# A gate matrix on its way through DRAM: eight groups of four expert blocks side by side behind the partition

## The chip, the cores and the metric

One core of one Trainium2 chip runs the program. The time is that of the device for one execution, in microseconds; lower is better. The kernel before was run three times (1939.65, 1940.6 and 1941.2 us, median 1940.6 us), and one more execution was profiled.

## The reference, cut to what matters

One decoder layer over 512 tokens of width 1024: a recurrent mixer and a sparse attention, merged; then a layer of 16,384 experts of which each token uses 8 heads x 16; then an embedding gate and a norm. The change lies in the layer of experts. For a token `t` with input `x`, expert scores are sums of two key scores, the best 16 of each head are kept, and their softmax is the gate:

```python
def peer_ffn(x, w_q, sub_keys, u_tab, v_tab):
    ...
    e_idx = (jnp.take_along_axis(i1, ci // PEER_TOPK, axis=-1) * N_KEYS +
             jnp.take_along_axis(i2, ci % PEER_TOPK, axis=-1))
    g = jax.nn.softmax(best, axis=-1).astype(x.dtype)
    ...
        act = jax.nn.gelu(jnp.einsum('cd,chkd->chk', xc, u)) * gc
        v = v_tab[ec]
        return jnp.einsum('chk,chkd->cd', act, v)
```

An expert is named by two numbers of 0 to 127: its block `e` (128 blocks of 128 experts) and its place in the block.

## The kernel before

The tokens stand in four tiles of 128. For three of them (384 tokens, `ND`) the kernel doesn't gather experts: it computes the activation of every expert for every token, `gelu(x u)`, block by block, multiplies it by a gate matrix G that is zero except at the chosen experts, and multiplies the result by the table `v`. For the fourth tile (`GT`) it gathers rows of both tables with indirect DMAs from GpSimd.

Three things run side by side from 798 to 1186 us, in one order written out by hand for each engine:

- *The activations of the blocks,* `xu_fill` (L1085): for each block `e`, a load of the table on SyncE's queue (L1060), a split into a high and a low part on ScalarE (`uh`, L1065) and VectorE (`ul`, L1070), 24 matmuls (`xu`), the gelu on ScalarE (`ac`, L1080), and a store of `ac` to `xdram` from ScalarE's queue (L1097).
- *The choice and the gate matrix,* `choose` (L1131), for one tile of tokens after another. First VectorE picks the experts. Then, eight tokens at a time, it builds one-hot matrices `oh` (L1238 and L1239); TensorE multiplies them (`G`, L1215), which gives 128 x 128 gates for a token; ScalarE copies them out of PSUM into `gst` (L1218), which is [place 128, block 128, token 32]. Every 32 tokens `gst` is stored to `gdram` from ScalarE's queue (L1221). There are 3 tiles x 4 such stores.
- *The gathers* of the fourth tile: rows come by GpSimd's indirect DMAs, VectorE multiplies them (L1267, L1273).

`choose` yields estimated costs, and the loop at L1287 hands out pieces of the activations and gathers against them, so how many blocks lie between two pieces of a tile's choice is fixed when the program is built.

The next stage is the loop at L1417 over the 128 blocks, TensorE's `va` matmuls (L131 to L133 by the helper `mm3`). For each block SyncE's queue loads the table `v` (L1107) and, for the blocks whose activations had been stored, `ac` from `xdram` (L1112). For each four blocks it loads their gates for all 384 tokens, `gt`, which is [place 128, 12 groups of 32 tokens, 4 blocks, 32 tokens] (`load_g`, L1311). VectorE multiplies (`a_mul`, L1325), both engines split (`split`, L125 and L128), and TensorE adds up. Blocks whose activations are not stored are computed there. The first `load_g` is issued behind the last store to `gdram`, and waits for it.

A DMA issue is an instruction of its engine: ScalarE's sequencer takes its own DMA issues in their order among the activations and copies, and what is behind an issue that is not yet accepted waits.

`gdram` before has the dimensions [32 groups of four blocks, 12 groups of 32 tokens, place 128, 4 blocks x 32 tokens]: for one group of blocks and one group of tokens a partition holds 128 numbers, which is 512 bytes. The tile `gst` is written as 32 such pieces for each of its 128 partitions, and `gt` is read as 12 such pieces for each partition.

Of the kernel before, what the change touches and what calls it, by code (L numbers as in the profile page):

```python
# [10 lines left out]
F32 = mybir.dt.float32  # L11
# [35 lines left out]
ND = GT * 128  # L47
NE = 128
# [45 lines left out]
def tile_hybrid(ctx, tc, a, out, dbg=None):  # L94
    nc = tc.nc
    V, A, T, G, SP = nc.vector, nc.scalar, nc.tensor, nc.gpsimd, nc.sync
# [7 lines left out]
    def enter(cm):  # L104
        return cm, cm.__enter__()
# [8 lines left out]
    def bank(name, tag="ax"):  # L114
        if tag == "ax":
            tag = "aaax"[turn[0] % 4]
            turn[0] += 1
        return ps.tile([128, 512], F32, name=name, tag=tag, bufs=NBK[tag])
# [23 lines left out]
    attcm, at = enter(tc.tile_pool(name="att", bufs=1, side="left"))  # L142
    p1cm, p = enter(tc.tile_pool(name="p1", bufs=2, side="right"))
    dr = ctx.enter_context(tc.tile_pool(name="dr", bufs=1, space=DRAM))
    gdram = dr.tile([NE // 4, ND // 32, 128, 128], F32, name="gdram")
    xdram = dr.tile([NE, 128, ND], F32, name="xdram")
    hdram = dr.tile([NT, 128, D], F32, name="hdram")
    x2dram = dr.tile([128, D], F32, name="x2dram")
# [674 lines left out]
    p2cm, p = enter(tc.tile_pool(name="p2", bufs=2, side="left"))  # L823
    for n in range(1, len(blocks) + 1):
# [5 lines left out]
        if n < len(blocks):  # L830
# [4 lines left out]
            i, hp = blocks[n]  # L835
# [24 lines left out]
    p3cm, p = enter(tc.tile_pool(name="p3", bufs=2, side="left"))  # L860
# [91 lines left out]
    p4cm, p = enter(tc.tile_pool(name="p4", bufs=1, side="left"))  # L952
# [149 lines left out]
    vring, vrs, gts = [], {}, {}  # L1102
# [28 lines left out]
    def choose(i, order):  # L1131
# [25 lines left out]
        g = gsel if i == GT else p.tile([128, 128], F32, name="g", tag="g")  # L1157
# [52 lines left out]
        def g_mm(oh, gst, t0):  # L1210
            for t1 in range(0, TB, 4):
                o = bank("G")
                for t in range(t1, t1 + 4):
                    for q in range(2):
                        T.matmul(o[:, (t - t1) * 128:(t - t1 + 1) * 128], oh[:, 1, t], oh[:, 2 + q, t],  # L1215
                                 start=q == 0, stop=q == 1)
                c = t0 % 32 + t1
                A.activation(gst[:, :, c:c + 4].rearrange("p a t -> p t a"), o.rearrange("p (t a) -> p t a", t=4),  # L1218
                             AF.Copy, scale=1.0 / GSC)
            if (t0 + TB) % 32 == 0:  # L1220
                A.dma_start(gdram[:, i * 4 + t0 // 32].rearrange("b p f -> p b f"),  # L1221
                             gst.rearrange("p (b a) t -> p b (a t)", a=4))

        pend = None
        for t0 in range(0, 128, TB):
            if t0 % 32 == 0:
                gst = p.tile([128, 128, 32], F32, name="gst", tag="gst", bufs=2)
            if t0 % (2 * TB) == 0:
                spread(t0 + 4 * TB)
            ptr = ptrs.pop(t0)  # L1230

            def bt(q):
                return ptr.rearrange("p (q t) r -> p q t r", q=4)[:, q:q + 2, :, None, :].to_broadcast([128, 2, TB, 128 // RUN, RUN])

            def runs(o):
                return o.rearrange("p q t (n r) -> p q t n r", r=RUN)
            oh = p.tile([128, 4, TB, 128], F16, name="oh", tag="oh", bufs=2)
            V.tensor_tensor(runs(oh[:, 0:2]), runs(iot[:, None, None, :].to_broadcast([128, 2, TB, 128])), bt(0), op=OP.is_equal)  # L1238
            V.tensor_tensor(runs(oh[:, 2:4]), runs(oh[:, 0:1].to_broadcast([128, 2, TB, 128])), bt(2), op=OP.mult)  # L1239
            if pend:  # L1240
                g_mm(*pend)
            pend = (oh, gst, t0)
            if i == order[-1]:
                ring_open(t0 // TB)
            yield 2450
        g_mm(*pend)

    BLK = 32
# [53 lines left out]
    p5cm, p = enter(tc.tile_pool(name="p5", bufs=2, side="left"))  # L1302
# [5 lines left out]
    def load_g(e):  # L1308
        if e % 4 == 0 and e < NE:
            gts[e // 4] = p.tile([128, ND // 32, 4, 32], F32, name="gt", tag="gt", bufs=2)  # L1310
            SP.dma_start(gts[e // 4].rearrange("p s a t -> p s (a t)"), gdram[e // 4].rearrange("s p f -> p s f"))  # L1311

    def loads(e):
        load_v(e)
        load_g(e)
        load_a(e)
# [87 lines left out]
    while nst[0] < nst0 + XTRA:  # L1404
        if nst[0] == nst0 + 2 and 0 not in vs:
            load_g(0)
            v_split(0)
        next(fillg)
# [162 lines left out]
```

## Time and profile before

| What | us |
|---|---|
| Median of 3 runs | 1940.6 |
| Lowest and highest | 1939.65, 1941.2 |
| The profiled execution | 1940.42 |
| Its span on the chip | 1938.7 |
| Busy in the span: TensorE | 1831.7 |
| Busy in the span: VectorE | 1432.9 |
| Busy in the span: ScalarE | 820.8 |
| Busy in the span: GpSimd | 602.1 |

Busy times are the union of the records of an engine's instructions; a DMA issue is not counted as busy, it has rows of its own under ACTq or SPq. PE is TensorE, PEld its loading of weights, DVE VectorE, ACT ScalarE, POOL GpSimd, SP SyncE. In a row of a group, `out<-in` names the tiles, `x` the count. A wait is written "engine, instruction <- what released it: total, times, longest". In the timeline a row has start, length and instruction, and in brackets the idle time before it. A granted clock of 1.00 is TensorE's full speed.

### The profile page before, as it was taken

The page shows a single profiled execution, that of the slowest core. Times are in us where ns is not written, and L with a number is a line of the kernel's source. Part 1 is how long each engine was busy: PE and PEld are TensorE (multiplying, and loading weights), DVE is VectorE, ACT ScalarE, POOL GpSimd, SP SyncE. Part 2 cuts the span into 40 slices and gives each one's busy share as a digit, 9 for nine tenths or more (in the row PEclk, how much of TensorE's full clock was granted, in tenths as well). Part 3 has the DMA queues.
Part 4 walks back from the last instruction along what each step waited for, and adds up shares of the span by engine and source line. Part 5 has one row for each costly group of instructions (what it writes and reads, how often), then busy time and mean ns, then how long its engine had stood idle before and what let it go on. Part 6 is the DMA issues. An engine that isn't in the chain of part 4 may idle for free.

```text
span 1938.7 us, 26466 instructions
## 1 busy us (share of the span) xinstructions
PE 1831.7 (94%) x9817; PEld 1599.4 (82%) x9817; DVE 1432.9 (74%) x2681; ACT 820.8 (42%) x1254; POOL 602.1 (31%) x381
## 2 busy tenths in 40 slices
PE   7988999999999999898999898999999999999997
PEld 6767888777779888888898887888888899999986
DVE  6887616666633389988999965878888788888864
ACT  4453323344422343573574563333333333333343
POOL 3443445321034303221222211222222255555400
PEclk9989999999999999999999999999999999999999
DMA  4353232211025437688797888999999899999951
GB/s 168 98 166 112 77 108 66 72 49 45 22 72 179 175 119 272 232 293 268 237 311 257 287 278 272 354 354 345 355 343 354 307 325 346 330 346 343 369 183 44
DMA packets 224578, 432.89 MB, mean 223 GB/s; under 512 B 14528, under 2 KB 136896, under 8 KB 224448
## 3 DMA queue, kind: packets, MB, share of 16 engines
q1 hardware_dynamic: 124128, 250.15, 38.0%
q0 software_dynamic: 37728, 137.38, 19.5%
q10 hardware_dynamic: 62592, 43.66, 6.9%
q8 instruction: 77, 1.26, 0.3%
q14 instruction: 53, 0.43, 0.1%
HBM read 382.05 MB, written 49.09 MB: 222 GB/s over the span
## 4 chain that ended last, share of the span: by engine, by line
PE 61%; DVE 19%; ACT 8%; ACTq 3%; issue 3%; DMA 1%; DVEq 0%
PE va L133 9%; PE va L131 9%; PE va L132 9%; PE xu L131 4%; PE xu L133 4%; PE xu L132 4%; ACT gst L1218 4%; ACTq L1097 3%; DVE ul L1070 3%; DVE gr L1267 1%; ACT uh L1065 1%; PE z_m L131 1%; PE z_w_a L131 1%; PE z_w_b L133 1%; PE z_w_a L132 1%
## 5 line engine op out<-in xcount | busy, mean ns | idle before, releaser
L131 PE MATMUL xu<-x2hi,uh 128*128 128x384 f32 x1008 | 348.8, 346 | 14.7 <-ACT ac L1080 14.7
L133 PE MATMUL xu<-x2hi,ul 128*128 128x384 f32 x1008 | 343.9, 341 | 12.3 <-DVE ul L1070 12.3
L132 PE MATMUL xu<-x2lo,uh 128*128 128x384 f32 x1008 | 342.4, 340 | 0.0
L1252 POOL DMA_INDIRECT gr<-in_peer_u,eidx x128 | 167.6, 1309 | 465.8 <-DVE gr L1267 304.6
L131 PE MATMUL va<-v,A 128*128 128x512 f32 x768 | 299.0, 389 | 1.5 <-ACT A L125 1.5
L133 PE MATMUL va<-v,A 128*128 128x512 f32 x768 | 299.2, 390 | 0.0
L132 PE MATMUL va<-v,A 128*128 128x512 f32 x768 | 298.8, 389 | 0.0
L1252 POOL DMA_INDIRECT gr<-in_peer_v,eidx x128 | 185.0, 1446 | 340.3 <-DVE acc L1273 270.0
L125 ACT CAST v<-vring 128x1024 fp32r<-128x1024 f32 x128 | 134.8, 1053 | 254.0 <-issue 162.2
L131 PEld LDWEIGHTS xu<-x2hi,uh 128*128 128x128 f32 x1008 | 193.8, 192 | 19.5 <-ACT ac L1080 17.8
L128 DVE TENSOR_TENSOR v<-vring,v 128x1024 fp32r<-128x1024 f32 x128 | 156.5, 1223 | 68.3 <-ACT v L125 68.0
L133 PEld LDWEIGHTS xu<-x2hi,ul 128*128 128x128 f32 x1008 | 193.4, 192 | 15.4 <-DVE ul L1070 15.4
L132 PEld LDWEIGHTS xu<-x2lo,uh 128*128 128x128 f32 x1008 | 193.7, 192 | 2.0
L1065 ACT CAST uh<-ur 128x1024 fp32r<-128x1024 f32 x126 | 132.2, 1050 | 123.7 <-issue 53.4
L1070 DVE TENSOR_TENSOR ul<-ur,uh 128x1024 fp32r<-128x1024 f32 x126 | 153.2, 1218 | 37.8 <-ACT uh L1065 31.1
L133 PEld LDWEIGHTS va<-v,A 128*128 128x128 f32 x768 | 144.1, 188 | 30.2 <-DVE A L128 0.3
L131 PEld LDWEIGHTS va<-v,A 128*128 128x128 f32 x768 | 144.1, 188 | 29.9 <-ACT A L125 1.8
L132 PEld LDWEIGHTS va<-v,A 128*128 128x128 f32 x768 | 144.2, 188 | 28.5
L1273 DVE SCALAR_TENSOR_TENSOR acc<-gr,dots,acc 128x1024 f32<-128x1024 f32 x128 | 163.8, 1280 | 1.5
L1267 DVE SCALAR_TENSOR_TENSOR gr<-gr,x2g 128x1024 f32<-128x1024 f32 x128 | 153.6, 1217 | 4.0 <-DMA gr<-in_peer_u,eidx 4.0
L1080 ACT ACTIVATE ac<-xu 128x384 f32<-128x384 f32 x128 | 64.1, 501 | 192.6 <-PE xu L133 188.5
L1218 ACT ACTIVATE gst<-G 128x512 f32<-128x512 f32 x96 | 97.7, 1140 | 8.4 <-PE G L1215 6.9
(446 smaller groups left out, 3568.5 us busy)
## 6 DMA issues: line engine op xcount, KB each, us to landing
vring<-in_peer_v SPq DMA_DIRECT2D x128, 512.0 KB, 6.2
ur<-in_peer_uT SPq DMA_DIRECT2D x126, 512.0 KB, 5.3
gdram<-gst ACTq DMA_DIRECT2D x12, 2048.0 KB, 11.2
gt<-gdram SPq DMA_DIRECT2D x32, 768.0 KB, 9.1
xdram<-ac ACTq DMA_DIRECT2D x87, 192.0 KB, 4.2
vring<-xdram SPq DMA_DIRECT2D x87, 192.0 KB, 8.0
raw_m<-in_w_in SPq DMA_DIRECT2D x16, 512.0 KB, 3.5
raw_rx<-in_w_in SPq DMA_DIRECT2D x8, 512.0 KB, 3.5
```

Source lines behind the costliest of these rows:

```text
L125: A.copy(hi, src)
L128: (eng or V).tensor_tensor(lo, src, f(hi), op=OP.subtract)
L131: T.matmul(o, sh, mh, start=start, stop=False)
L132: T.matmul(o, sh, ml, start=False, stop=False)
L133: T.matmul(o, sl, mh, start=False, stop=stop)
L1065: A.copy(us[e][0], urs[e])
L1070: V.tensor_tensor(us[e][1], urs.pop(e), f(us[e][0]), op=OP.subtract)
L1080: A.activation(ac, o[:, :ND], AF.Gelu_apprx_tanh)
L1218: A.activation(gst[:, :, c:c + 4].rearrange("p a t -> p t a"), o.rearrange("p (t a) -> p t a", t=4), AF.Copy, scale=1.0 / GSC)
L1252: G.indirect_dma_start(out=r, out_offset=None, in_=tab, in_offset=bass.IndirectOffsetOnAxis(ap=eidx[:, j:j + 1], axis=0))
L1267: V.scalar_tensor_tensor(r, r, 1.0, x2g, op0=OP.mult, op1=OP.mult, accum_out=dots[:, j:j + 1])
L1273: V.scalar_tensor_tensor(acc, r, dots[:, j:j + 1], acc, op0=OP.mult, op1=OP.add)
```

## The change

The dimension of the blocks is cut in two: `gdram` becomes [4 sets of 32 blocks, 12 groups of 32 tokens, place 128, 8 groups of four blocks, 4 blocks x 32 tokens]. Behind a partition now stand eight groups of four blocks, 1024 numbers or 4 KB, side by side. The store writes 4 such pieces for each partition. The load of four blocks takes from each partition's 4 KB the 512 bytes of its group: 12 pieces of 512 bytes for each partition, as many as before, from other addresses. The size of the DRAM tile, the tiles in SBUF and the order of all instructions stay.

```diff
-    gdram = dr.tile([NE // 4, ND // 32, 128, 128], F32, name="gdram")
+    gdram = dr.tile([NE // 32, ND // 32, 128, 8, 128], F32, name="gdram")
...
             if (t0 + TB) % 32 == 0:
-                A.dma_start(gdram[:, i * 4 + t0 // 32].rearrange("b p f -> p b f"),
-                             gst.rearrange("p (b a) t -> p b (a t)", a=4))
+                A.dma_start(gdram[:, i * 4 + t0 // 32].rearrange("b p g f -> p b (g f)"),
+                            gst.rearrange("p (b a) t -> p b (a t)", a=32))
...
             gts[e // 4] = p.tile([128, ND // 32, 4, 32], F32, name="gt", tag="gt", bufs=2)
-            SP.dma_start(gts[e // 4].rearrange("p s a t -> p s (a t)"), gdram[e // 4].rearrange("s p f -> p s f"))
+            SP.dma_start(gts[e // 4].rearrange("p s a t -> p s (a t)"), gdram[e // 32, :, :, e // 4 % 8].rearrange("s p f -> p s f"))
```

## The prediction

> **What bounds the kernel now.** I read the page first: its span, the chain that ended last, and the table of DMA issues with the queue of ScalarE (q10) above it.
>
> ```profile
> span 1938.7 us, 26466 instructions
> q10 hardware_dynamic: 62592, 43.66, 6.9%
> PE 61%; DVE 19%; ACT 8%; ACTq 3%; issue 3%; DMA 1%; DVEq 0%
> PE va L133 9%; PE va L131 9%; PE va L132 9%; PE xu L131 4%; PE xu L133 4%; PE xu L132 4%; ACT gst L1218 4%; ACTq L1097 3%; DVE ul L1070 3%; DVE gr L1267 1%; ACT uh L1065 1%; PE z_m L131 1%; PE z_w_a L131 1%; PE z_w_b L133 1%; PE z_w_a L132 1%
> gdram<-gst ACTq DMA_DIRECT2D x12, 2048.0 KB, 11.2
> gt<-gdram SPq DMA_DIRECT2D x32, 768.0 KB, 9.1
> ```
>
> TensorE carries the chain, but 3% of it (some 60 us) is an entry that computes nothing: ACTq at L1097, ScalarE's sequencer busy issuing the small store of `ac` to `xdram`. The change doesn't touch L1097; it touches the 12 stores to `gdram` (L1221) on the same queue. Each is cut by the old layout into 128 partitions times 32 pieces of 512 bytes, 4096 pieces; 12 of them are 49,152 of q10's 62,592 packets. Next, the view of line L1097, and ScalarE's timeline around the first and the last of the 12 stores (start, length, instruction; in brackets the idle time before it).
>
> ```profile
> L1097 ACTq DMA_DIRECT2D xdram<-ac x87: 326/326/7565, 698.9 to 1183.2; - x87
> ```
> ```profile
> 818.13 0.38 ACTq L1221 DMA_DIRECT2D gdram<-gst  x1
> 818.61 0.49 ACT L1080 ACTIVATE ac<-xu 128x384 f32<-128x384 f32 x1 [0.51 <-ACT gst L1218]
> 819.13 4.22 ACTq L1097 DMA_DIRECT2D xdram<-ac  x1
> 823.39 1.05 ACT L1065 CAST uh<-ur 128x1024 fp32r<-128x1024 f32 x1 [4.29 <-issue]
> ...
> 1157.40 0.38 ACTq L1221 DMA_DIRECT2D gdram<-gst  x1
> 1157.88 0.49 ACT L1080 ACTIVATE ac<-xu 128x384 f32<-128x384 f32 x1 [0.51 <-ACT gst L1218]
> 1158.40 7.57 ACTq L1097 DMA_DIRECT2D xdram<-ac  x1
> 1166.01 1.04 ACT L1065 CAST uh<-ur 128x1024 fp32r<-128x1024 f32 x1 [7.64 <-issue]
> ```
> ```profile
> ACT uh L1065 <- issue: 53.4, 10, 7.6
> ```
>
> A normal L1097 issue takes 0.326 us. The one that comes next after an L1221 takes 4.22 us the first time and 7.57 us the last, and ScalarE stands still behind it. I read this as the queue being held until the 4096 pieces ahead are mostly taken. The list of waits puts 10 such stalls at 53.4 us; all 12 long issues add up to 61.9 us, 57.9 us above 12 normal ones.
>
> That is not yet time of the kernel. The stage from 798 to 1186 us has three stretches in which G is computed, with two in between where VectorE picks the experts. Busy times by stretch (columns: length, PE, PEld, DVE, ACT, POOL, granted clock, DMA share, GB/s):
>
> ```profile
> 798.00:884.00 86.00, 74.33 (x584) 69.78 (x583) 73.68 (x120) 56.26 (x76) 18.94 (x12) 1.00 0.86 283
> 884.00:944.00 60.00, 56.18 (x313) 54.97 (x312) 59.06 (x220) 24.38 (x37) 14.84 (x10) 0.97 0.69 231
> 944.00:1024.00 80.00, 74.27 (x580) 70.44 (x579) 72.81 (x108) 54.57 (x71) 17.72 (x11) 0.98 0.90 298
> 1024.00:1084.00 60.00, 53.59 (x291) 51.90 (x290) 59.80 (x208) 23.33 (x34) 16.18 (x10) 0.94 0.71 243
> 1084.00:1186.00 102.00, 89.77 (x645) 84.95 (x643) 68.33 (x60) 60.74 (x79) 13.84 (x9) 0.95 0.84 277
> ```
>
> The stretches between are VectorE's (59.06 of 60 and 59.80 of 60 us): nothing is won there. In the three others TensorE is busy for 74.33 of 86, 74.27 of 80 and 89.77 of 102 us. While ScalarE is stuck, TensorE works on what lies ready, so most of the 57.9 us is covered. What it waits for ScalarE, asked stretch by stretch (total us, times, longest; two rows each for 798 to 884, 944 to 1024 and 1084 to 1186):
>
> ```profile
> PE xu L131 <- ACT ac L1080: 5.5, 4, 2.8
> PE G L1215 <- ACT gst L1218: 2.7, 3, 2.3
> ...
> PE G L1215 <- ACT gst L1218: 2.1, 2, 1.8
> PE xu L131 <- ACT ac L1080: 2.0, 2, 1.5
> ...
> PE G L1215 <- ACT gst L1218: 6.2, 6, 2.6
> PE xu L131 <- ACT ac L1080: 4.4, 3, 3.5
> ```
>
> That makes 8.2, 4.1 and 10.6 us. Idle TensorE costs a second time: the stretches of 4 us around two of these waits, in the columns of above, show the granted clock drop behind them.
>
> ```profile
> 984.00:988.00 4.00, 1.92 (x16) 1.57 (x15) 1.85 (x2) 2.93 (x4) 0.00 (x0) 1.00 1.06 343
> 988.00:992.00 4.00, 3.97 (x19) 3.97 (x19) 3.96 (x4) 3.60 (x6) 0.76 (x1) 0.57 1.02 362
> ...
> 1164.00:1168.00 4.00, 0.51 (x3) 0.51 (x3) 0.00 (x0) 1.59 (x3) 0.00 (x0) 0.75 0.91 284
> 1168.00:1172.00 4.00, 4.00 (x14) 4.00 (x13) 1.89 (x2) 3.37 (x4) 0.00 (x0) 0.50 0.57 171
> ```
>
> By the clocks of the whole stretches, 0.98 and 0.95, this slowness is worth 0.02 x 74.27 = 1.5 us and 0.05 x 89.77 = 4.5 us, and nothing in the first.
>
> **The change part by part.** No instruction is added, removed or moved, on any engine or queue, and no wait: same 12 stores, 32 loads, bytes and tiles.
>
> *The store.* Per partition 4 pieces of 4 KB replace 32 of 512 bytes: 512 pieces instead of 4096. No 2 MB store of 4 KB pieces is issued on ScalarE's queue in this trace. The nearest row is SyncE's: four loads `xt`, back to back, 512 pieces of 4 KB and 2 MB together.
>
> ```profile
> L237 SPq DMA_DIRECT2D xt<-in_x x4: 390/420/654, 0.8 to 2.1; - x4
> ```
>
> All four were accepted within 2.1 + 0.65 - 0.8 = about 2 us, none over 0.654 us, though they landed after 3.8 to 9.7 us by the same view. So such a queue takes 512 pieces without being held. Bounds for the 57.9 us: if pieces count, nearly all of it goes; if bytes count, only the shorter transfer helps. For that, the transfer rate in 40 slices from 835 to 852 us, a window that holds one store:
>
> ```profile
> GB/s 279 351 274 109 0 0 0 11 304 348 347 348 348 347 348 348 348 351 266 220 339 422 334 342 318 310 364 356 336 383 410 425 431 383 316 151 47 87 67 77
> ```
>
> I read the plateau of 348 as the store alone, and 425 to 431 as 4 KB loads. If pieces of 4 KB bring the store to 425, it shortens by 18%, and 10 us of ScalarE's stall would go. I take the first bound, because `xt` is the same count and size of pieces.
>
> A rule of the Trainium skill speaks against this term: "DMA: Bandwidth & Descriptors", section "Issuing engines are not separate DMA queues", holds the sequencer's time for starting a DMA to be usually small beside the transfer. By it the issue would be worth nothing and the sum would be about 0; L1097's 7.57 us against 0.326 us contradicts it here.
>
> *What is late next.* With the stalls gone, TensorE may win at most 8.2 us, 4.1 + 1.5 = 5.6 us and 10.6 + 4.5 = 15.1 us: 28.9 us. In the first two stretches VectorE stands close behind (73.68 and 72.81 us, as full as TensorE within 1.5 us), and the one-hots and `ul` pass between these engines in order through two and three buffers; I take two thirds: 5.5 and 3.7 us. In the third VectorE has 33.7 us free; I take nine tenths, 13.6 us. The tenth kept back is the path to the first `va`: the last store must land, block 0 of G be read back, multiplied and split.
>
> ```profile
> SPq L1311 <- DMA gdram<-gst: 11.6, 1, 11.6
> ```
>
> That wait of 11.6 us, the load's 9.1 us and the product end at about 1180 us, near the last `xu`; if the store lands no sooner, they cap the gain there by 1 to 3 us.
>
> Sum: 5.5 + 3.7 + 13.6 = 22.8 us. The profiled execution took 1940.4 us (span 1938.7 and 1.7 around it), 0.2 us below the median of 1940.6: 1940.6 - 22.8 = 1917.8 us.
>
> *The load.* `load_g` still reads 1536 pieces of 512 bytes, but the pieces of neighbouring partitions now lie 4 KB apart, not end to end, and those of one partition 512 KB apart, not 64 KB. I cost this at nothing, and name its cover: the last stage, where TensorE is full.
>
> ```profile
> 1300.00:1500.00 200.00, 200.00 (x885) 165.58 (x884) 163.56 (x213) 72.46 (x101) 48.32 (x48) 1.00 0.99 348
> ```
> ```profile
> 1268.65 0.33 SPq L1107 DMA_DIRECT2D vring<-in_peer_v  x1
> ...
> 1284.97 0.33 SPq L1107 DMA_DIRECT2D vring<-in_peer_v  x1
> ```
>
> Four blocks take 16.3 us and move 348 GB/s x 16.3 us = 5.7 MB, 0.79 MB of it `gt`. At 425 GB/s the same bytes take 13.4 us, at the mean rate of now all 16.3; I take 2 us of slack. `gt` at 348 GB/s is 2.3 us, so it may grow to 4.3 us, about half its rate, before the loads are late. Ends: below nothing by the same 2 us at best, which TensorE hides; above, see the third rival. No row here reads 512-byte pieces 4 KB apart; the nearest is the old store itself, with 512-byte pieces of a partition 768 KB apart, at 348 GB/s.
>
> **The rivals.**
>
> *One: the queue is held by bytes, or VectorE takes back what TensorE wins.* By bytes 10 of 57.9 us go and TensorE's share is 10/57.9 x 28.9 = 5 us: 1935.6. For it: all the long issues end while the store still moves. Against it: `xt`. With VectorE taking all but the third stretch's first half, some 7 us: 1933. 14 in 100, half of it within 0.2%.
>
> *Two: the chain is right,* and all 57.9 us are the kernel's: 1882.7. Against it: TensorE has only 29.6 us of idle time in the three stretches. 5 in 100 for anything under 1907.
>
> *Three: slower.* Reads 4 KB apart meet on few memory banks, and the last stage becomes one of loads. It decides from half the present rate, and eats the whole gain where a group of four blocks is 22.8/21 = 1.1 us late (21 groups until block 87), near 150 GB/s. At a third (116 GB/s) `gt` takes 6.8 us, 2.5 late, 53 us in all: 1971. For it: a DMA share of 0.99 there. Against it: the pieces of a partition were never adjacent, and the scattered store runs full. 9 in 100 for slower.
>
> The same page, section "Latency and other measured facts", has large powers of two as row pitch cost bandwidth: 103 GB/s at 4 MiB, but 207 at 512 KiB, and the full rate again with 4 KiB added. By its worst figure reads would halve and the time stay near 1920; by its 512 KiB figure nothing happens. No run here shows it yet.
>
> **How the numbers follow.** The forecast, 1917.8, holds if the stalls go and the loads hold: between half the gain of the waits (11.5 us, 1929) and the whole 28.9 us with a little of the transition (1907): 70 in 100. Between 1929 and 1936.7: 8 (half of rival one, and loads a little late). Within 0.2% (3.9 us, about what a measurement of this kernel can tell from no change): 8. Slower: 9. Under 1907: 5. Faster is 70 + 8 + 5 = 83. The range 1907 to 1936 holds 78 of 100.
>
> **What would show it.** Right: L1097 without an issue over about 1 us; "uh waits for issue" gone from the list; q10 down by 43,008 packets; the three stretches shorter by 5, 4 and 13 us, the two between unchanged; the clock near 1.00 after 1084 us; 16.3 us per four blocks as before. Wrong: long L1097 issues remain (bytes), the stretches keep their length with TensorE waiting for one-hots (VectorE), or `vring` products wait for `gt` and TensorE idles after 1186 us (reads).

## The result, and the profile after

The changed kernel took 1911.16 us (median of 4 runs, 1906.13 to 1914.94) against 1940.9 us before in the same comparison: a ratio of 0.9831, with a 95% interval of 0.9801 to 0.9862. The forecast was 1917.8 us with a range of 1907 to 1936. The profiled execution took 1911.14 us.

First the page, in the rows that answer to those of before.

```profile
span 1909.4 us, 26466 instructions
q10 hardware_dynamic: 19584, 43.66, 6.1%
PE 52%; DVE 26%; DMA 8%; issue 4%; ACT 4%; SPq 0%; DVEq 0%; ACTq 0%; POOL 0%
PE va L131 7%; PE va L132 7%; PE va L133 7%; DMA ur<-in_peer_uT 4%; DVE ul L1070 4%; PE xu L131 3%; PE xu L133 3%; PE xu L132 3%; DVE acc L1273 2%; DMA wgr<-in_ple_wg 2%; DVE gr L1267 2%; DVE v L128 1%; DVE oh L1238 1%; PE G L1215 1%; PE z_m L131 1%
gdram<-gst ACTq DMA_DIRECT2D x12, 2048.0 KB, 9.2
gt<-gdram SPq DMA_DIRECT2D x32, 768.0 KB, 9.2
```

ScalarE's queue has the same bytes in 43,008 packets fewer, as counted ahead. ACTq has gone from 3% to 0% of the chain, and `gst` (L1218) has left it; VectorE (19% to 26%) and loads (DMA, 1% to 8%) have more of it. The store lands after 9.2 us, not 11.2, and the load as before. The view of line L1097, and ScalarE's timeline at the first and the last of the twelve stores:

```profile
L1097 ACTq DMA_DIRECT2D xdram<-ac x87: 326/327/856, 699.8 to 1150.1; - x87
```
```profile
818.66 0.38 ACTq L1221 DMA_DIRECT2D gdram<-gst  x1
819.14 0.49 ACT L1080 ACTIVATE ac<-xu 128x384 f32<-128x384 f32 x1 [0.51 <-ACT gst L1218]
819.67 0.34 ACTq L1097 DMA_DIRECT2D xdram<-ac  x1
820.05 1.05 ACT L1065 CAST uh<-ur 128x1024 fp32r<-128x1024 f32 x1 [0.41 <-ACT ac L1080]
...
1127.04 0.38 ACTq L1221 DMA_DIRECT2D gdram<-gst  x1
1127.56 0.49 ACT L1080 ACTIVATE ac<-xu 128x384 f32<-128x384 f32 x1 [0.56 <-PE xu L133]
1128.09 0.33 ACTq L1097 DMA_DIRECT2D xdram<-ac  x1
```

The issue behind the store is now as short as any other: 0.34 and 0.33 us, where 4.22 and 7.57 us had stood. Its longest is 0.856 us.

Where did the 29 us come from? The stage is cut here at events of the program, not at round times: the first one-hot (L1238), the last store of each of the three tiles (L1221), the first one-hot of the next, and the first product of gates (L1325). So row by row the two tables hold nearly the same work; TensorE's counts differ by up to 14 matmuls in a row, since its work is not cut at ScalarE's stores. Columns: bounds, length, busy PE, PEld, DVE, ACT, POOL, granted clock, DMA share, GB/s. Before:

```profile
799.63:872.61 72.98, 65.05 (x533) 60.82 (x531) 67.12 (x92) 51.54 (x69) 16.76 (x10) 1.00 0.84 276
872.61:942.14 69.53, 61.97 (x342) 60.44 (x343) 62.67 (x243) 27.21 (x38) 15.77 (x11) 0.98 0.75 252
942.14:1013.65 71.51, 67.29 (x541) 63.78 (x540) 68.50 (x87) 53.15 (x71) 16.78 (x10) 0.98 0.86 287
1013.65:1081.18 67.53, 61.12 (x331) 59.43 (x330) 63.14 (x228) 25.30 (x35) 17.12 (x11) 0.95 0.76 256
1081.18:1157.40 76.22, 67.45 (x537) 63.44 (x536) 62.85 (x54) 50.66 (x67) 13.84 (x9) 0.98 0.88 297
1157.40:1179.76 22.36, 18.87 (x96) 18.55 (x95) 5.87 (x6) 7.74 (x11) 0.00 (x0) 0.85 0.88 266
sum 380.13, PE 341.75 PEld 326.45 DVE 330.15 ACT 215.59 POOL 80.27; mean PE 56.96 PEld 54.41 DVE 55.03 ACT 35.93 POOL 13.38
```

After:

```profile
800.19:864.84 64.65, 61.47 (x520) 58.47 (x519) 64.10 (x80) 52.34 (x69) 15.11 (x9) 1.00 0.83 310
864.84:931.11 66.27, 63.61 (x356) 62.72 (x355) 65.37 (x256) 27.44 (x38) 18.23 (x12) 0.97 0.75 265
931.11:996.46 65.35, 63.47 (x531) 60.54 (x531) 64.80 (x70) 54.38 (x71) 15.09 (x9) 1.00 0.82 301
996.46:1063.32 66.86, 61.21 (x340) 60.04 (x339) 66.69 (x245) 25.53 (x35) 19.53 (x12) 0.96 0.77 272
1063.32:1127.04 63.72, 63.13 (x526) 60.30 (x526) 61.09 (x53) 52.15 (x67) 15.09 (x9) 0.99 0.91 343
1127.04:1146.57 19.53, 18.64 (x108) 18.32 (x107) 7.00 (x6) 7.77 (x11) 0.00 (x0) 1.00 0.90 316
sum 346.38, PE 331.52 PEld 320.39 DVE 329.06 ACT 219.60 POOL 83.04; mean PE 55.25 PEld 53.40 DVE 54.84 ACT 36.60 POOL 13.84
```

The stage is 33.75 us shorter, 380.13 to 346.38 us. The three tiles' gates win 8.3, 6.2 and 12.5 us, the two choices between 3.3 and 0.7 us, the way to the last stage 2.8 us. TensorE's idle time in it falls from 38.4 to 14.9 us, and its busy time from 341.75 to 331.52 us for nearly the same matmuls (2380 and 2381 records); the clock column of the last two stretches goes from 0.98 and 0.85 to 0.99 and 1.00. VectorE's idle time falls from 50.0 to 17.3 us. What TensorE and VectorE waited for in this stage, before and after (total us, times, longest):

```profile
PE xu L131 <- ACT ac L1080: 14.7, 10, 3.5
PE G L1215 <- ACT gst L1218: 11.1, 11, 2.6
PE G L1215 <- DVE oh L1239: 6.5, 5, 1.5
...
DVE ul L1070 <- ACT uh L1065: 26.1, 9, 6.0
```
```profile
PE G L1215 <- DVE oh L1239: 5.6, 6, 1.5
PE xu L133 <- DVE ul L1070: 4.4, 3, 2.5
PE xu L131 <- ACT ac L1080: 2.7, 1, 2.7
```

TensorE's waits for ScalarE fall from 25.8 to 2.7 us. VectorE's 26.1 us behind ScalarE's `uh` are gone from its list.

The other parts of the run change little in sum. The first one-hot comes 0.6 us later than before. From the first product of gates to the last (1179.8 to 1870.9 us before, 1146.6 to 1842.6 us after) the last stage is 4.9 us longer, and the end behind it 1.0 us shorter: 0.6 - 33.8 + 4.9 - 1.0 = -29.3 us, the difference of the spans. The 4.9 us are a question of their own, below.

### The profile page after: what moved, and what is told of

Read it like the earlier page. It is cut to its first block, busy times and chain, and to the rows that moved or that the text cites. A ratio compares the mean times of both kernels' runs of the same rounds, so it can differ in the third digit from the quotient of the medians.

```text
span 1909.4 us, 26466 instructions
## 1 busy us (share of the span) xinstructions
PE 1823.9 (96%) x9817; PEld 1592.6 (83%) x9817; DVE 1430.7 (75%) x2681; ACT 821.5 (43%) x1254; POOL 601.7 (32%) x381
## 4 chain that ended last, share of the span: by engine, by line
PE 52%; DVE 26%; DMA 8%; issue 4%; ACT 4%; SPq 0%; DVEq 0%; ACTq 0%; POOL 0%
PE va L131 7%; PE va L132 7%; PE va L133 7%; DMA ur<-in_peer_uT 4%; DVE ul L1070 4%; PE xu L131 3%; PE xu L133 3%; PE xu L132 3%; DVE acc L1273 2%; DMA wgr<-in_ple_wg 2%; DVE gr L1267 2%; DVE v L128 1%; DVE oh L1238 1%; PE G L1215 1%; PE z_m L131 1%
## 5 line engine op out<-in xcount | busy, mean ns | idle before, releaser
L131 PE MATMUL xu<-x2hi,uh 128*128 128x384 f32 x1008 | 344.8, 342 | 3.3 <-ACT ac L1080 2.7
L1252 POOL DMA_INDIRECT gr<-in_peer_v,eidx x128 | 182.7, 1427 | 335.5 <-DVE acc L1273 267.7
L1218 ACT ACTIVATE gst<-G 128x512 f32<-128x512 f32 x96 | 100.2, 1158 | 15.5 <-PE G L1215 15.4
```

The lines of the kernel that those rows point to most:

```text
L131: T.matmul(o, sh, mh, start=start, stop=False)
L1252: G.indirect_dma_start(out=r, out_offset=None, in_=tab, in_offset=bass.IndirectOffsetOnAxis(ap=eidx[:, j:j + 1], axis=0))
```

## The experiments

**Theory:** what the old store cost was ScalarE's queue, held while 4096 pieces were taken; the number of pieces, not the bytes. The loads at the new addresses cost nothing. **Rivals:** the loads cost the 4.9 us of the last stage; many small pieces slow everything, whoever issues them; the bytes hold the queue.

In what follows "the stage" is the time from the first one-hot to the first product of gates (380.1 us before, 346.4 after), and "the tail" that from the product of gates of block 87, the first whose activations are computed in the last stage, to the product of block 127 (330.6 us before, 335.5 after).

### The changed kernel again

> The changed kernel once more, beside the three others of this job, with five rounds. Its profile differed from the forecast in one place: from the first product of gates (1146.6 us) to the last, the last stage took 4.9 us longer than before, and its gt loads behind block 87 landed after about 12.4 us in place of 9.3. If that is a property of the layout, this profile shows it again (a last product of gates 696 us behind the first, landing over 11 us). If it is chance, the distance is 691 us, as before, in at least some of the profiles of this layout. Time by both: 1906 to 1915 us.

Ratio 0.9839 (0.9817 to 0.9862), median 1910.46 us against 1942.99. The stage is 345.9 us, from the first product to the last 693.4 us, the tail 333.0 us, and `gt` landed after 8.9 us (median) to 12.7 us (longest) in it. So the gain of the stage repeats within 0.4 us, and the length of the tail doesn't: it lies between the two values that were foreseen.

### The two halves of the change, each alone

The new store with loads at the old addresses, and the old store with loads at the new ones: two views of one flat DRAM tile.

```diff
+    gflat = dr.tile([NE * 128 * ND], F32, name="gdram")
+    gdram = gflat.rearrange("(s j p g f) -> s j p g f", s=NE // 32, j=ND // 32, p=128, g=8)
+    gold = gflat.rearrange("(b j p f) -> b j p f", b=NE // 4, j=ND // 32, p=128)
...
-gdram[e // 32, :, :, e // 4 % 8].rearrange("s p f -> p s f")
+gold[e // 4].rearrange("s p f -> p s f")
```

> The new stores (4 pieces of 4 KB for each partition), but the loads take the addresses of the old layout: 12 pieces of 512 bytes 64 KB apart for each partition, neighbouring partitions end to end. The loads so bring gates of other experts. Theory A (the loads 4 KB apart cost 5 us in the last stage): the stage from 798 us is as short as in the changed kernel, the last stage is 691 us from the first to the last product of gates, gt lands after about 9 us behind block 87, time near 1906 us. Rival B (the 5 us come from another cause, such as how loads, gathers and blocks fall together after an earlier start): 696 us, landing near 12.4 us, time as the changed kernel.

> The other half alone: the old stores (32 pieces of 512 bytes), and the loads at the addresses of the new layout, 512 bytes out of every 4 KB, which bring gates of other experts. Theory A: all twelve long issues at L1097 are there again, no gain before 1186 us, gt lands after over 11 us behind block 87, and the time is about 5 us above the kernel before: 1946 us. Rival B: landing about 9 us, time as the kernel before within 2 us.

| Kernel | Ratio to before | Stage, us | Tail, us | `gt` landed in the tail, us (median, longest) |
|---|---|---|---|---|
| before | 1 | 380.1 | 330.6 | 9.3, 11.0 |
| changed, first profile | 0.9831 (0.9801 to 0.9862) | 346.4 | 335.5 | 12.2, 13.6 |
| new store alone | 0.9838 (0.9816 to 0.9860) | 346.3 | 331.0 | 9.0, 10.9 |
| new addresses of the loads alone | 0.9991 (0.9974 to 1.0007) | 378.8 | 331.5 | 9.0, 12.4 |

The store is the whole gain. The loads alone change nothing that the timing can tell, and the 5 us that theory A of these two runs gave them (1946 us) are not there: 1939.18 us against 1942.99. In the view of its line the old store's hold is back (the line is 1099 in this kernel):

```profile
L1099 ACTq DMA_DIRECT2D xdram<-ac x87: 325/326/7505, 702.5 to 1186.5; - x87
```

### The old store from another queue

```diff
-                A.dma_start(gdram[:, i * 4 + t0 // 32].rearrange("b p f -> p b f"),
+                SP.dma_start(gdram[:, i * 4 + t0 // 32].rearrange("b p f -> p b f"),
```

> The old layout as a whole; only the twelve stores to gdram are issued from SyncE's queue in place of ScalarE's. Theory (ScalarE's queue was held while 4096 pieces were taken, and nothing else of the store cost time): no issue at L1097 is longer than about 1 us, ScalarE's wait before uh is gone; SyncE's next load of the table is held for 5 to 10 us instead, of which its buffers cover some: between 1908 and 1930 us. Rival (the transfer of many small pieces slows everything, whoever issues it): TensorE's waits stay and the time is within 4 us of the kernel before.

Ratio 0.9832 (0.9808 to 0.9855), 1909.53 us: as good as the new layout, with all the pieces of 512 bytes. The stage is 346.5 us. The small pieces as such cost nothing that the timing can tell; what cost was whose queue they stood in. Three views of this kernel: the lines L1097 and L1060 (SyncE's loads of the table), and ScalarE's waits in the stage.

```profile
L1097 ACTq DMA_DIRECT2D xdram<-ac x87: 325/326/358, 703.2 to 1154.6; - x87
```
```profile
L1060 SPq DMA_DIRECT2D ur<-in_peer_uT x66: 327/328/7555, 809.5 to 1148.0; - x66
```
```profile
ACT uh L1065 <- DMA ur<-in_peer_uT: 18.9, 12, 4.1
```

The hold has moved: now an issue of SyncE's is up to 7.555 us long. SyncE only loads, and its loads run some blocks ahead; of the holds, ScalarE feels 12 waits of 18.9 us in all for the late table, and TensorE waits as little as in the changed kernel. I had left room up to 1930 us for such waits; there was no need of it.

### One size changed: how many pieces

The same layout with two, four and 32 groups side by side in place of eight (in the case of two). Each ran once: 1911.81, 1907.36 and 1905.96 us against 1941.81 us before, so what is read here is the stage and the issues, not the time.

```diff
-    gdram = dr.tile([NE // 32, ND // 32, 128, 8, 128], F32, name="gdram")
+    gdram = dr.tile([NE // 8, ND // 32, 128, 2, 128], F32, name="gdram")
...
-                            gst.rearrange("p (b a) t -> p b (a t)", a=32))
+                            gst.rearrange("p (b a) t -> p b (a t)", a=8))
...
-gdram[e // 32, :, :, e // 4 % 8]
+gdram[e // 8, :, :, e // 4 % 2]
```

> Two groups of four blocks side by side: 16 pieces of 1 KB for each partition, 2048 for a store. Theory A (a queue takes about 1.2 ns for each piece, whatever its size, as the shortest hold of the old store, 5.0 us for 4096, says): accepted about 2.5 us behind the store, so the next issue at L1097 is 1.5 to 2.5 us long, and the stage from the first one-hot to the first product of gates lies between 346 and 360 us (380 before, 346 with 4 KB). Theory B (the queue has room for some 2000 pieces, and is held only for those above it until others have left): no issue over 0.9 us, stage 346 us. Theory C (bytes): about 7 us, 380 us.

> Four groups side by side: 8 pieces of 2 KB for each partition, 1024 for a store. Theory A: accepted 1.3 us behind the store, where L1097 comes 1.0 us behind it, so no issue over about 0.9 us; stage 346 to 348 us. Theory B: the same. Theory C (bytes): about 7 us, 380 us.

> All 32 groups side by side: one piece of 16 KB for each partition, 128 for a store; the loads take 512 bytes out of every 16 KB. Theories A and B: no issue at L1097 over 0.9 us, stage 346 us. If loads at a wide pitch cost time in the last stage, its part behind block 87, 330 to 331 us in the three profiles with the old addresses and 331.5 to 335.5 us in the three with 4 KB, is over 333 us here and gt lands after over 12 us at the latest; if not, under 332 us.

The line L1097 in the kernels with 1 KB, 2 KB and 16 KB, in this order:

```profile
L1097 ACTq DMA_DIRECT2D xdram<-ac x87: 326/326/5470, 696.4 to 1153.3; - x87
```
```profile
L1097 ACTq DMA_DIRECT2D xdram<-ac x87: 326/326/461, 699.4 to 1149.6; - x87
```
```profile
L1097 ACTq DMA_DIRECT2D xdram<-ac x87: 326/326/1088, 698.1 to 1148.4; - x87
```

And ScalarE's timeline at two stores, the third of the second tile before and the third of the third tile with 1 KB, where the next issue ends soonest among the stores that held one:

```profile
997.95 0.38 ACTq L1221 DMA_DIRECT2D gdram<-gst  x1
998.43 2.09 ACT L1218 ACTIVATE gst<-G 128x512 f32<-128x512 f32 x2 [0.51 <-ACT gst L1218]
1000.30 0.54 ACT L1080 ACTIVATE ac<-xu 128x384 f32<-128x384 f32 x1
1000.87 2.09 ACTq L1097 DMA_DIRECT2D xdram<-ac  x1
```
```profile
1114.29 0.38 ACTq L1221 DMA_DIRECT2D gdram<-gst  x1
1114.77 0.49 ACT L1080 ACTIVATE ac<-xu 128x384 f32<-128x384 f32 x1 [0.51 <-ACT gst L1218]
1115.29 1.35 ACTq L1097 DMA_DIRECT2D xdram<-ac  x1
```

| Pieces of a store | Stage, us | Next issue over, from the store's start: soonest, latest of the held ones, us | Longest issue at L1097, us |
|---|---|---|---|
| 4096 of 512 bytes | 380.1 | 5.0, 10.6 | 7.57 |
| 2048 of 1 KB | 353.1 | 2.4, 6.5 | 5.47 |
| 1024 of 2 KB | 346.7 | not held | 0.46 |
| 512 of 4 KB | 346.4 | not held | 0.86 |
| 128 of 16 KB | 345.3 | not held | 1.09 |

Half the pieces with the same bytes, half the shortest hold: 5.0 and 2.4 us. Bytes (380 us) and a room for 2000 pieces (no hold with 2048) are both refuted. Theory A of these three runs, 1.2 ns for each piece, fits the two shortest holds (5.0 us/4096, 2.4 us/2048) and the lengths of the stage. But A had named 1.5 to 2.5 us as the length of the held issues, and of the eight that were held two took 4.01 and 5.47 us. So there is a part above the shortest hold, up to 5.6 us with 4096 pieces and 4.1 us with 2048, which the count of pieces doesn't give.

The DMA packets show what does. Here are the packets that ScalarE's queue (q10) started from the start of a store to the end of the issue that it held (packets, MB, share of the 16 engines' time): a short and a long hold before, at 997.95 us (5.01 us) and 853.58 us (10.40 us), then the shortest and the longest with 1 KB, at 1114.29 us (2.35 us) and 1094.86 us (6.47 us). Up to 128 packets in each may be those of a store of `ac`.

```profile
q10 hardware_dynamic: 2708, 1.39, 91.5%
q10 hardware_dynamic: 2689, 1.43, 44.8%
q10 hardware_dynamic: 505, 0.52, 61.7%
q10 hardware_dynamic: 475, 0.49, 21.2%
```

Holds of very different length end at nearly the same count. The store at 853.58 us only starts its pieces after 4.76 us, the one at 997.95 us after 0.94 us; the holds end with 1483 and 1389 of their 4096 pieces not yet started, and those with 1 KB with 1540 and 1599 of 2048. Of the 32 holds on ScalarE's queue in these traces (twelve before, twelve with the loads' new addresses, eight with 1 KB) 28 end with 968 to 1599 pieces of the store waiting, four with 350 to 782; the twelve on SyncE's queue above end with 362 to 1291. The loads of `gt` on SyncE's queue, 1536 pieces each, speak against a time for each piece as well: 1.2 ns would make 1.8 us, but here, before, the next issue was over 1.19 us behind the load's start, when none of its pieces had started (the first did after 3.48 us).

```profile
1589.71 0.43 SPq L1311 DMA_DIRECT2D gt<-gdram  x1
1590.19 0.71 SPq L1060 DMA_DIRECT2D ur<-in_peer_uT  x1
```

So the traces fit theory B of these runs better, with room for some 1500 to 1600 pieces in place of 2000: the queue is held at least until all but that many have started, and a hold is long where the store's pieces start late or leave slowly. This is read from the traces above; no run was made to test it, and why some holds last beyond that point is open.

With 1024 pieces the next issue, 1.0 us behind the store, is never held, though at the store of 964.41 us none of the pieces had started when that issue was over; from there on nothing is left to win by larger pieces, for this neighbour. The longest issue with 16 KB, 1.09 us, is over the 0.9 us that was named; it is one of 87, and the second profile of that layout has none over 0.41 us.

### The 4.9 us of the last stage

Four runs ask whether the loads' pitch makes the tail longer: a layout with nine places of 512 bytes behind each partition, eight of them used, so that partitions lie 4.5 KB apart, profiled once and then timed; the changed kernel a third time; the layout with 16 KB once more. A fifth puts the load of `gt` behind that of the table.

```diff
+    gdram = dr.tile([NE // 32, ND // 32, 128, 9, 128], F32, name="gdram")
...
+                A.dma_start(gdram[:, i * 4 + t0 // 32, :, 0:8].rearrange("b p g f -> p b (g f)"),
```

> The changed layout with nine places of 512 bytes behind each partition, of which eight are used: pieces of 4 KB as before, 4.5 KB from partition to partition and 576 KB from one group of tokens to the next. Stage 346 us. If the power of two in the loads' pitch makes the part behind block 87 longer, it is 330 to 331 us here, and gt lands after 11.3 us at the latest; if any wide pitch or chance does, between 331.5 and 335.5 us is as likely.

> The changed kernel a third time. The part of the last stage behind block 87 was 335.5, 333.0 and 331.5 us in the profiles that load 512 bytes out of every 4 KB, and between 330.1 and 333.1 us in the seven others. If the 4 KB pitch is the cause, this profile has over 331.2 us and gt lands after over 11.3 us at the latest. If it is chance, a value from 330 to 331 us is the likelier one. Time 1905 to 1914 us.

> The layout with nine places of 512 bytes behind each partition once more. If the 4 KB pitch is the cause of the longer part behind block 87: 330 to 331 us here, gt landed after at most 11.3 us, and a median 1 to 4 us under the changed kernel's in this job. If chance: the same spread in both, medians within 2 us.

> One piece of 16 KB for each partition, timed: by the theory of the pieces it stands level with the changed kernel in the stage from 798 us (345 to 346.5 us), since 512 pieces are no longer held either; loads 16 KB apart would show behind block 87 (over 331.2 us) if pitch mattered. Median within 3 us of the changed kernel's in this job.

```diff
     def loads(e):
         load_v(e)
-        load_g(e)
         load_a(e)
...
             u_load(e + 3)
+        load_g(e + 3)
```

> The changed layout; in the last stage gt is issued behind the loads of ac and of the table u for the same block, in place of ahead of them. In the slow profile the table's load lands after 13 to 15 us in every fourth block, and ScalarE's uh waits for it; the chain goes through it. If the longer part behind block 87 is made there: 330.1 us or less and uh waits for ur under 25 us in all, whatever gt does; median 1 to 4 us under the changed kernel's in this job. If not: as the changed kernel.

| Kernel | Median, us (runs) | Ratio to before | Stage, us | Tail, us | `gt` landed in the tail, longest, us |
|---|---|---|---|---|---|
| 4.5 KB pitch | 1906.13 (1) | | 346.4 | 330.1 | |
| changed, third time | 1908.27 (5) | 0.9829 (0.9808 to 0.9851) | 346.2 | 330.2 | 11.4 |
| 4.5 KB pitch again | 1911.94 (5) | 0.9829 (0.9803 to 0.9855) | 346.4 | 332.4 | 14.4 |
| 16 KB pieces again | 1905.03 (5) | 0.9818 (0.9795 to 0.9841) | 345.3 | 330.7 | 12.6 |
| table ahead of `gt` | 1908.76 (5) | 0.9825 (0.9804 to 0.9845) | 345.9 | 330.1 | 14.6 |

The changed kernel's tail is 330.2 us this time, after 335.5 and 333.0 us; with the padded pitch it is 330.1 us once and 332.4 us the other time; with the widest pitch 330.9 and 330.7 us. The old addresses gave 330.1 to 331.0 us, and 1 KB pieces 333.1 us. No pitch goes with the long tail. The first six profiles had looked as if 4 KB did; the later ones took that away. So the 4.9 us go with the execution and not with the layout, as far as one to three profiles of each can show.

The first profile has the longest tail. From the list of all waits, after and with the table's load put first:

```profile
ACT uh L1065 <- DMA ur<-in_peer_uT: 56.2, 15, 7.4
```
```profile
ACT uh L1065 <- DMA ur<-in_peer_uT: 9.8, 6, 2.8
```

In the longest tail ScalarE waits for the table that stands behind `gt` on SyncE's queue. The load of `gt` holds that queue too: the table's issue right behind it took up to 4.30 us in the tail before and up to 5.29 us in this one. With the table ahead, none of the table's issues in the tail took over 1.45 us, `gt` landed as late as ever (13.3 us by the median, 14.6 at the longest) and `uh` waited for 9.8 us only, the least of all profiles; the tail was 330.1 us. That fits, but one profile of a thing that comes by chance doesn't show it, and the median is level with the changed kernel's. Over the other profiles this wait doesn't go with the tail: it is 27.2 us in all where the tail took 333.0 us, and 38.0 us where it took 330.7 us. TensorE's idle time in the tail does: none up to 331.5 us, 0.2 us at 332.4 us, 0.6 us at 333.0 and 333.1 us, 2.0 us at 335.5 us; but that is less than half of what the tail is longer. What makes the rest, and why `gt` lands late in some executions, stays open.

No layout tried is surely better than the changed one: the 16 KB pieces have the lowest median, 1905.03 us, but their interval and that of the changed kernel overlap almost wholly.

## Why the prediction was right, and what was off

*The queue held by pieces: right.* "If pieces count, nearly all of it goes": all twelve long issues went, and of the two bounds (57.9 us or 10 us of ScalarE's time) the first held. The row of the four `xt` loads, the same count and size on another queue, was the right neighbour to take. The reading behind it, a queue held until the 4096 pieces are "mostly taken", is what the packets show: at the end of the twelve holds 2584 to 3546 pieces had started.

*The gain is TensorE's waiting, not the 57.9 us of the queue: right in kind.* The second rival (1882.7 us) is refuted: with the holds gone the stage gained 33.8 us. TensorE's waits for ScalarE, 22.9 us of rows ahead, fell to 2.7 us.

*The clock: near in size, with a part left over.* The forecast gave the slow clock 1.5 + 4.5 = 6.0 us. By the clock columns of the two tables the sum of busy time times lost clock is 9.8 us before and 5.0 us after, so 4.8 us went. But TensorE's busy time in the stage shrank by 10.2 us. The rest, some 5 us, I can't assign; fewer stops of the pipelined matmuls would do it, but that is argued and not shown.

*What is late next: the step that failed.* "In the first two stretches VectorE stands close behind", two thirds were taken; of the stretches between it said "nothing is won there". Forecast for the three stretches: 5.5, 3.7 and 13.6 us, 22.8 in sum. With each choice counted to the gates ahead of it and the transition to the third, they won 11.6, 6.8 and 15.3 us, 33.8 in sum. I had compared the two engines' busy times and kept back a third for the fuller one. But VectorE stood still in the same holds: 26.1 us in 9 waits for `uh`, a row that the forecast doesn't count. One of them, 6.0 us, lay behind the first tile's last store, at the head of a choice that is VectorE's alone; so time was won there too. The cause of both idle times went, and both engines closed up, so the second half of the first rival, that VectorE takes back what TensorE wins (1933 us), did not come either; after the change VectorE is busy for 64.10 of 64.65 us and 64.80 of 65.35 us in the first two tiles. The full 28.9 us of my own ceiling would have been the better forecast, and even that was short of the 33.8 us, mostly in TensorE's busy time (6.0 us against 10.2 us; its idle time fell by 23.5 us, against 22.9 us of waits). So the forecast time lay 6.6 us above the measured one, inside the range.

*The load at nothing: right.* The ring of the last stage (87 blocks with stored activations) took 351.5 us before, 351.5 us after, and 351.5 to 351.6 us in every profile of every pitch. The rule of the Trainium skill ("DMA: Bandwidth & Descriptors", section "Latency and other measured facts") that large powers of two as row pitch cost bandwidth is given there for 512 KiB and more from partition to partition. With 4, 4.5 and 16 KB from partition to partition and 512-byte pieces no cost showed here; the larger pitches were not tried. The section "Issuing engines are not separate DMA queues" of the same page of the Trainium skill calls the sequencer's time for starting a DMA usually small beside the transfer. That does not hold here: an issue of a store of `ac` took up to 7.57 us, and such a store landed 4.2 us after its issue began by the median, and putting the large store on another engine's queue saved as much as the new layout.

*The path to the first `va`:* the tenth kept back for it was not needed. The stores landed 2 us sooner by the median, and the transition was 2.8 us shorter.

## What to carry to other kernels

Look for long DMA issues on the queue of an engine that also computes, and ask what stood ahead of them in that queue: here the one that was long was the victim, and the cause was the transfer with many pieces just before it. Cut that transfer into fewer pieces (1024 were few enough here), or issue it from a queue whose other work runs ahead. To price such a stall, ask every engine what it waited for in it; two engines that stood still in the same stall did not hold each other back here when it went.

## What the runs showed of the hardware

- Behind a store of many pieces the next issue on the same queue was held, for the same bytes, the longer the more pieces there were: at the soonest 5.0 us from the store's start with 4096 pieces, 2.4 us with 2048, not at all with 1024. Of 32 holds on ScalarE's queue none ended with more than 1599 pieces waiting, and 28 with 968 to 1599. SyncE's queue was held for up to 7.555 us by the same store of 4096 pieces. The other queue goes on meanwhile: the loads of the table that SyncE issued during ScalarE's holds took 0.33 us each before, but for one of 0.752 us (1.42 us with the loads' new addresses).
- The part of a hold above the shortest, up to 5.6 us, comes where the pieces start late (at 853.58 us 4.76 us behind the store's start, at 997.95 us 0.94 us) or leave slowly (at 1099.75 us the first started after 0.89 us, and the hold was over after 10.63 us).
- 512-byte pieces 4 KB, 4.5 KB or 16 KB apart from partition to partition were read without any loss that 351.5 us of a stage with a DMA share of 0.99 would show.
- Executions of one kernel differ by up to 14 us (1933.23 to 1947.35 us for the kernel before in one comparison). In the profiles of all the variants the first one-hot came between 796.0 and 806.3 us, and the tail took 330.1 to 335.5 us. What lies between, the stage, repeated within 0.6 us (345.9 to 346.5 us) in the eight profiles with stores in 4 KB pieces or with the old store on SyncE's queue.
